# A network kernel on one core, with its list scheduler driven by the time-line model

## The chip, the cores and the metric

The kernel runs on one core of one Trainium2 chip. A core has TensorE (PE in the profile; its weight loads are PEld), VectorE (DVE), ScalarE (ACT), GpSimd (POOL) and SyncE (SP), which here issues DMAs. Each engine works through its own queue of instructions in order and waits on semaphores for the others. The metric is device time in microseconds of one execution; the kernel before takes 3337.39 us in the median of three runs (3337.23 to 3337.42).

## What is computed

The input x is 512 tokens by 1024 channels, float32. Four blocks follow one another; each has a mixer and a feed-forward part, joined by residual adds and RMS norms:

- layer 0: dilated attention (8 heads, three branches) beside latent attention with low-rank queries and keys; then a gated feed-forward network, modulated by six vectors that come from `silu(c) @ ada_w`;
- layer 1: a spatial gating unit beside a 2-D neighbourhood attention (8 heads); then a gated feed-forward network;
- block 2: an RWKV-7 time mix (16 heads of 64) beside a conformer convolution (31 taps along the tokens), with gates;
- block 3: mLSTM heads (4) and differential attention heads (4), a per-layer embedding, and a feed-forward network with a convolution.

The recurrence of block 2 is, per head, with k̂ the normalised key:

```
S_t = S_{t-1} diag(w_t) - (S_{t-1} k̂_t)(k̂_t * a_t)^T + v_t k_t^T
y_t = S_t r_t          # then a group norm per head, a bonus term and a gate
```

The kernel computes it in 8 chunks of 64 tokens. Within a chunk everything is matrix products, once a small triangular system has been inverted; from chunk to chunk the state S must be carried in order.

## The kernel before

Activations are held transposed, channels on partitions, as tiles of 128x512. Every weight matrix is streamed from HBM in slabs by SP's DMAs (L108). A slab is split in two reduced-precision parts, `whi` (a cast on ACT, L117) and `wlo` (a subtraction on DVE or POOL, L118), and each product takes three matmuls on PE (L123, L124, L125, with the activation split alike in `hhi` and `hlo`). "GEMM matmul" below means one of these three. They accumulate in PSUM tiles `psg`.

Block 2 handles the RWKV heads in pairs, p = 0 to 7. One pair has three parts:

- `rwkv_prep` makes the operands of its 8 chunks.
- `rwkv_invert` sends the triangular blocks through DRAM into another layout (`dram_L` to `uL`, L1147 and L1157), inverts them in some 20 small DVE steps (L1171, L1172), sends the result back through DRAM (`dram_DT<-uX`), and finishes on PE (`ps_D` L1211, `ps_T` L1217, `ps_X` L1225).
- `rwkv_steps` walks the chunks. One chunk is a chain over three engines: PE `ps_v` (L1248, L1250 with the state S), a copy of one half on DVE (L1251) and of the other on ACT (L1252) into `zV`, PE `ps_u` (L1255), ACT copy into `VU` (L1256), PE `ps_s` (L1259), DVE update of S (L1261). PE also adds to the output `ps_y` (L1253, L1264). After the eighth chunk comes the group norm: 8 squares on ACT (L1273), a row of small DVE operations (L250 to L256, L1276), 8 scalings on ACT (L1278), and four PE transposes `ps_yt` (L1281), read by DVE (L1283).

While these chains wait, other work is to fill the engines ("filler"): the conformer's input product and its 30 taps per channel tile on DVE (L1305, on tiles `z`), and the gates' products. The program lists them per pair in a string (`order`) and gives them a lower priority, by `high_priority(offset=self.fill_offset)` with an offset of -3000. The same device is used in layer 0, layer 1 and block 3, where attention heads run beside the next projection's or the gates' products. In block 3 a head's score block is: PE `ps_s` (L1635), DVE minimum (L1639), ACT exponential (L1641), a product on POOL (L1647), a sum on DVE (L1648), PE transposes `ps_pt` (L1651), an ACT copy (L1653), PE `ps_pv` (L1656); after four blocks come a head norm and transposes `ps_hdt` (L1619).

None of the queues' orders is written out by hand. The program records instructions in program order with their dependencies and priorities. A list scheduler then orders them: it steps a simulated machine through time, and whenever an engine is free there, it gives it the instruction of highest priority among those that are ready. A few manual edges (`issue_after`) tie fillers to a place. So the orders depend on what the simulated machine says is ready, and when.

## Time and profile before

| | |
|---|---|
| median of three runs | 3337.39 us |
| the profiled execution | 3332.78 us |
| its span (first to last instruction) | 3331.0 us |
| PE busy | 3179.2 us (95%) |
| DVE busy | 2041.3 us (61%) |
| ACT busy | 1386.5 us (42%) |
| POOL busy | 515.1 us (15%) |
| mean granted clock of PE | 0.983 of full speed |

A busy time is the union of an engine's instructions. Matmuls overlap one another in the pipeline, so their own durations sum to more than the busy time. The granted clock is 1.00 when PE runs at 2.4 GHz and 0.50 when it runs at 1.2 GHz; a stretch's figure is a mean of the two.

### The profile page before, as it was taken

How to read it: one execution, taken by the hardware profiler on the slowest of the kernel's cores; microseconds unless marked ns; L12 is line 12 of the kernel's file. 1: busy time of each engine (PE TensorE's matmuls, PEld its weight loads, DVE VectorE, ACT ScalarE, POOL GpSimd, SP SyncE). 2: the span in 40 equal slices, each digit the busy share in tenths (PEclk: the TensorE clock that was granted, in tenths of full speed). 3: DMA queues.
4: the chain of work that ended last, by engine and by line, in shares of the span. 5: the costliest groups of instructions: out<-in, count | busy, mean ns of one | idle time of the engine just before them, and what ended most of it. 6: DMA issues, size and time to landing. Idle time of an engine off the chain costs nothing. (4 is left out here: it accounts for less than half of the span.)

```text
span 3331.0 us, 43197 instructions
## 1 busy us (share of the span) xinstructions
PE 3179.2 (95%) x15337; PEld 2471.1 (74%) x15337; DVE 2041.3 (61%) x4002; ACT 1386.5 (42%) x2784; POOL 515.1 (15%) x603
## 2 busy tenths in 40 slices
PE   8999999999999999898899889999999999999998
PEld 6755778788778887666666656788877777788887
DVE  4576764654665356688778875434367764575665
ACT  3466332333443233454444444433244553343444
POOL 1000010111211011222223323111010011110111
PEclk9999999999999999999999999999999999999999
DMA  4411553525223332322122343233233125332322
GB/s 134 120 62 50 172 169 128 176 97 149 68 83 95 100 97 76 103 63 68 52 68 66 101 134 113 85 96 95 95 92 112 55 84 164 110 95 95 95 95 82
DMA packets 275032, 332.60 MB, mean 100 GB/s; under 512 B 52956, under 2 KB 188058, under 8 KB 274817
## 3 DMA queue, kind: packets, MB, share of 16 engines
q1 hardware_dynamic: 237392, 301.43, 29.4%
q10 hardware_dynamic: 33489, 12.39, 1.5%
q0 software_dynamic: 3936, 16.03, 1.5%
q8 instruction: 121, 1.98, 0.2%
q14 instruction: 94, 0.77, 0.1%
HBM read 311.88 MB, written 23.89 MB: 101 GB/s over the span
## 5 line engine op out<-in xcount | busy, mean ns | idle before, releaser
L118 DVE TENSOR_TENSOR wlo<-raw,whi 128x512 fp32r<-128x512 f32 (+2 forms) x865 | 625.2, 734 | 752.7 <-PE psg L124 419.3
L123 PE MATMUL psg<-hhi,whi 128*128 128x512 f32 (+1 forms) x2624 | 1044.5, 401 | 36.4 <-DVE glu L1301 7.0
L125 PE MATMUL psg<-hhi,wlo 128*128 128x512 f32 (+1 forms) x2624 | 1038.9, 397 | 13.3 <-DVE wlo L118 7.9
L124 PE MATMUL psg<-hlo,whi 128*128 128x512 f32 (+1 forms) x2624 | 1041.2, 397 | 0.0
L117 ACT CAST whi<-raw 128x512 fp32r<-128x512 f32 (+2 forms) x975 | 581.7, 604 | 1072.6 <-PE psg L124 924.6
L123 PEld LDWEIGHTS psg<-hhi,whi 128*128 128x128 f32 (+1 forms) x2624 | 496.5, 189 | 162.8 <-issue 17.2
L125 PEld LDWEIGHTS psg<-hhi,wlo 128*128 128x128 f32 (+1 forms) x2624 | 496.7, 189 | 124.9 <-POOL wlo L118 9.6
L124 PEld LDWEIGHTS psg<-hlo,whi 128*128 128x128 f32 (+1 forms) x2624 | 497.1, 189 | 107.2 <-issue 7.6
L123 PE MATMUL psg<-hidhi,whi 128*128 128x512 f32 x784 | 308.4, 394 | 1.0 <-DVE ffu L574 0.8
L125 PE MATMUL psg<-hidhi,wlo 128*128 128x512 f32 x784 | 308.0, 393 | 0.0
L124 PE MATMUL psg<-hidlo,whi 128*128 128x512 f32 x784 | 305.9, 390 | 0.0
L1305 DVE SCALAR_TENSOR_TENSOR z<-glu,par_B,z 128x512 f32<-128x512 f32 x240 | 197.0, 835 | 1.5
L118 POOL TENSOR_TENSOR wlo<-raw,whi 128x512 fp32r<-128x512 f32 (+1 forms) x110 | 146.8, 1341 | 281.3 <-ACT whi L117 217.3
L125 PEld LDWEIGHTS psg<-hidhi,wlo 128*128 128x128 f32 x784 | 147.2, 188 | 34.0
L124 PEld LDWEIGHTS psg<-hidlo,whi 128*128 128x128 f32 x784 | 147.2, 188 | 33.4
L123 PEld LDWEIGHTS psg<-hidhi,whi 128*128 128x128 f32 x784 | 147.4, 188 | 32.8 <-DVE ffu L574 1.3
L581 POOL TENSOR_TENSOR ffu<-ffu,ffg 128x512 f32<-128x512 f32 x44 | 64.7, 1469 | 582.6 <-DVE ffu L574 582.6
L1374 POOL TENSOR_TENSOR ffr<-ffr 128x512 f32<-128x512 f32 x32 | 40.1, 1261 | 293.0 <-ACT ffr L1373 286.9
L194 ACT CAST hidhi<-ffu 128x512 fp32r<-128x512 f32 x66 | 41.0, 622 | 106.1 <-POOL ffu L581 66.2
L195 DVE TENSOR_TENSOR hidlo<-ffu,hidhi 128x512 fp32r<-128x512 f32 x66 | 57.3, 868 | 30.9 <-ACT hidhi L194 29.4
L765 DVE SCALAR_TENSOR_TENSOR adacc<-adraw,c_act,adacc 128x1024 f32<-128x1024 f32 x42 | 53.9, 1284 | 33.4 <-DMA adraw<-in_ada_w_dram 33.0
L209 POOL TENSOR_TENSOR ss<-ss,sq 128x512 f32<-128x512 f32 x24 | 35.2, 1467 | 218.1 <-ACT sq L208 202.0
(572 smaller groups left out, 4040.3 us busy)
## 6 DMA issues: line engine op xcount, KB each, us to landing
raw<-in_ffn_w_gu_dram SPq DMA_DIRECT2D x176, 256.0 KB
raw<-in_w_in_dram SPq DMA_DIRECT2D x59, 512.0 KB
adraw<-in_ada_w_dram SPq DMA_DIRECT2D x48, 512.0 KB
raw<-in_w_up_dram SPq DMA_DIRECT2D x88, 256.0 KB
raw<-in_ffn_w_down_dram SPq DMA_DIRECT2D x42, 512.0 KB
raw<-in_w_ff_in_dram SPq DMA_DIRECT2D x32, 512.0 KB
raw<-in_w_ff_out_dram SPq DMA_DIRECT2D x32, 512.0 KB
raw<-in_w_in_dram SPq DMA_DIRECT2D x96, 128.0 KB
```

What stands on the lines that cost most here:

```text
L117: nc.scalar.copy(oi(hi), ri(r))
L118: eng.tensor_tensor(out=oi(lo), in0=ri(r), in1=fr(oi(hi)), op=ALU.subtract)
L123: first = nc.tensor.matmul(ps, lhsT=whi, rhs=xhi, start=start, stop=False)
L124: nc.tensor.matmul(ps, lhsT=whi, rhs=xlo, start=False, stop=False)
L125: nc.tensor.matmul(ps, lhsT=wlo, rhs=xhi, start=False, stop=stop)
L194: nc.scalar.copy(hi, t)
L195: nc.vector.tensor_tensor(out=lo, in0=t, in1=fr(hi), op=ALU.subtract)
L209: (nc.gpsimd if c < 4 else nc.vector).tensor_tensor(out=ss, in0=ss, in1=sq, op=ALU.add)
L581: nc.gpsimd.tensor_tensor(out=t, in0=t, in1=part[c], op=ALU.mult)
L765: nc.vector.scalar_tensor_tensor(out=acc, in0=raw, scalar=c[:, k:k + 1], in1=acc, op0=ALU.mult, op1=ALU.add)
L1305: tap = nc.vector.scalar_tensor_tensor(out=z[i], in0=g[:, j:j + T], scalar=cw(j), in1=z[i], op0=ALU.mult, op1=ALU.add)
L1374: nc.gpsimd.tensor_tensor(out=t, in0=t, in1=t, op=ALU.mult)
```

## The change

One argument is added where the program's context is made. The list scheduler then orders all queues with a time-line model of the engines, in place of its usual simulated machine.

```
-    with tile.TileContext(nc) as tc:
+    with tile.TileContext(nc, schedule_with_timeline_sim=True) as tc:
```

The two programs hold the same matmuls, vector operations and DMAs (PE 13741, DVE 4001, POOL 608, SP 943 instructions in both); what differs is the order in the queues, the waits that follow from it, and the number of ACT table loads (47, where it was 35). Three places show the kind of move.

On PE, in the fifth RWKV group (p = 4), from the `ps_u` of one chunk towards that of the next. Before:

```order
L1255 MATMUL ps_u_14484<-zV1_10969,zD0_10970 64x128
L123 MATMUL psg_15457<-hhi3_10779,whi_15498 128x512
L124 MATMUL psg_15457<-hlo3_10780,whi_15498 128x512
L125 MATMUL psg_15457<-hhi3_10779,wlo_15499 128x512
L1259 MATMUL ps_s_14487<-VU_14223,KB_14210 128x128
L1264 MATMUL ps_y_14458<-VU_14223,MLR_14180 64x64 x2
L123 MATMUL psg_15458<-hhi2_10773,whi_15494 128x512
L124 MATMUL psg_15458<-hlo2_10774,whi_15494 128x512
L125 MATMUL psg_15458<-hhi2_10773,wlo_15495 128x512
L123 MATMUL psg_15458<-hhi3_10779,whi_15498 128x512
L1248 MATMUL ps_v_14496<-VU_14223,MLR_14180 64x64 x2
L1250 MATMUL ps_v_14496<-S_14417,ar_14173 64x64 x2
```

And after, from the same `ps_u` (14484) on:

```order
L1255 MATMUL ps_u_14484<-zV1_10969,zD0_10970 64x128
L1259 MATMUL ps_s_14487<-VU_14223,KB_14210 128x128
L1264 MATMUL ps_y_14458<-VU_14223,MLR_14180 64x64 x2
L1248 MATMUL ps_v_14496<-VU_14223,MLR_14180 64x64 x2
L1250 MATMUL ps_v_14496<-S_14417,ar_14173 64x64 x2
L1253 MATMUL ps_y_14495<-S_14417,ar_14173 64x128
L1255 MATMUL ps_u_14504<-zV0_10968,zD0_10970 64x128
L1259 MATMUL ps_s_14507<-VU_14223,KB_14210 128x128
L1264 MATMUL ps_y_14495<-VU_14223,MLR_14180 64x64 x2
```

The GEMM matmuls on `psg` that stood in every gap of the chain are gone from this place. They now stand in blocks of about 20 in the gaps of the first chunks of the group. Counted over the eight groups, 34 of the 56 steps from one chunk to the next have no GEMM matmul in between (3, 3, 5, 3, 5, 4, 7 and 4 by group); before there was none of that kind.

On DVE, in the same group, from one `zV` copy to the next. Before, steps of the next pair's inversion stand there:

```order
L1251 COPY zV0_10968<-ps_v_14496 64x64
L1171 TENSOR_TENSOR uT_14891<-uX_14883,uM_14892 128x384
L1172 TENSOR_REDUCE uX_14883<-uT_14891 128x6x8
L1171 TENSOR_TENSOR uT_14891<-uX_14883,uL_14882 128x384
L1261 SCALAR_TENSOR_TENSOR S_14417<-S_14417,GC_13997,ps_s_14507 64x64 x2
L1172 TENSOR_REDUCE uX_14883<-uT_14891 128x2x8
L1251 COPY zV1_10969<-ps_v_14513 64x64
```

After, the same stretch holds seven convolution taps:

```order
L1251 COPY zV0_10968<-ps_v_14496 64x64
L1305 SCALAR_TENSOR_TENSOR z6_10986<-glu_15125,par_B_5986,z6_10986 128x512
L1305 SCALAR_TENSOR_TENSOR z7_10987<-glu_15128,par_B_5986,z7_10987 128x512
L1305 SCALAR_TENSOR_TENSOR z6_10986<-glu_15125,par_B_5986,z6_10986 128x512
L1305 SCALAR_TENSOR_TENSOR z7_10987<-glu_15128,par_B_5986,z7_10987 128x512
L1261 SCALAR_TENSOR_TENSOR S_14417<-S_14417,GC_13997,ps_s_14507 64x64 x2
L1305 SCALAR_TENSOR_TENSOR z6_10986<-glu_15125,par_B_5986,z6_10986 128x512
L1305 SCALAR_TENSOR_TENSOR z7_10987<-glu_15128,par_B_5986,z7_10987 128x512
L1305 SCALAR_TENSOR_TENSOR z6_10986<-glu_15125,par_B_5986,z6_10986 128x512
L1251 COPY zV1_10969<-ps_v_14513 64x64
```

The inversion of a pair now stands a whole group earlier (that of pair p+2 behind the group norm of pair p). Runs of three or four taps on each side of the state update stand in 13 of the 34 steps without GEMM matmuls (groups 0, 2 and 4); in the other 21, DVE has little beside the chain.

On PE, at the end of block 3's attention heads (`ps_s`, `ps_pt`, `ps_pv` and `ps_hdt` belong to the heads). Before:

```order
L1651 MATMUL ps_pt_23626<-ident_81,dP_23611 128x128 x3
L123 MATMUL psg_22468<-hhi6_20641,whi_22575 128x512
L124 MATMUL psg_22468<-hlo6_20642,whi_22575 128x512
L125 MATMUL psg_22468<-hhi6_20641,wlo_22576 128x512
L1656 MATMUL ps_pv_23632<-dv_20704,dPT_23630 128x128 x3
L123 MATMUL psg_22468<-hhi7_20645,whi_22579 128x512
L124 MATMUL psg_22468<-hlo7_20646,whi_22579 128x512
L125 MATMUL psg_22468<-hhi7_20645,wlo_22580 128x512
L1651 MATMUL ps_pt_23656<-ident_81,dP_23641 128x128 x4
L123 MATMUL psg_22469<-hhi6_20641,whi_22575 128x512
L124 MATMUL psg_22469<-hlo6_20642,whi_22575 128x512
L125 MATMUL psg_22469<-hhi6_20641,wlo_22576 128x512
```

After:

```order
L1656 MATMUL ps_pv_23603<-dv_20704,dPT_23601 128x128 x2
L1619 MATMUL ps_hdt_23400<-ident_81,hd_tm_23399 128x128 x4
L1651 MATMUL ps_pt_23626<-ident_81,dP_23611 128x128 x3
L1656 MATMUL ps_pv_23632<-dv_20704,dPT_23630 128x128 x3
L1651 MATMUL ps_pt_23656<-ident_81,dP_23641 128x128 x4
L1656 MATMUL ps_pv_23663<-dv_20704,dPT_23661 128x128 x4
L1619 MATMUL ps_hdt_23552<-ident_81,hd_tm_23551 128x128 x4
L123 MATMUL psg_23821<-hhi4_23717,whi_23827 128x512
L124 MATMUL psg_23821<-hlo4_23718,whi_23827 128x512
L125 MATMUL psg_23821<-hhi4_23717,wlo_23828 128x512
L123 MATMUL psg_23821<-hhi5_23721,whi_23831 128x512
L124 MATMUL psg_23821<-hlo5_23722,whi_23831 128x512
```

Before, the gates' GEMM matmuls stand between the last blocks, and some 260 more behind them. After, these have gone ahead of the heads' second half, the last ten blocks stand without them, and the next GEMM in the queue is one that reads the heads' results. In layer 1, in the same way, 24 of the 32 blocks of the neighbourhood attention (L711, L726, L738) stand without GEMM matmuls.

## Rows read from the trace of the kernel before

**Rows 1.** The page, part 1: busy time, share of the span, instructions.

```profile
PE 3179.2 (95%) x15337; PEld 2471.1 (74%) x15337; DVE 2041.3 (61%) x4002; ACT 1386.5 (42%) x2784; POOL 515.1 (15%) x603
```

**Rows 2.** Busy time by stage: stretch, length, engines, PEclk, DMA share, GB/s.

```profile
0.00:1312.00 1312.00, 1276.40 (x5837) 991.54 (x5837) 745.12 (x1333) 513.71 (x949) 140.41 (x148) 1.00 0.36 112
1312.00:1427.00 115.00, 96.39 (x497) 74.36 (x497) 81.01 (x169) 49.92 (x83) 33.45 (x60) 0.90 0.29 84
1427.00:2051.00 624.00, 554.28 (x3452) 398.80 (x3450) 495.40 (x1069) 302.71 (x798) 178.86 (x201) 0.95 0.29 82
2051.00:2112.00 61.00, 58.94 (x261) 47.27 (x261) 28.06 (x43) 20.07 (x36) 19.56 (x15) 1.00 0.32 99
...
2580.00:2760.00 180.00, 177.12 (x839) 132.85 (x838) 122.86 (x444) 91.35 (x253) 17.78 (x26) 1.00 0.24 70
```

**Rows 3.** What PE waited for: us in total, times, longest.

```profile
PE ps_u L1255 <- ACT zV L1252: 18.6, 7, 5.9
```

**Rows 4.** Time line of one chunk, last group: start, us, engine, line, operation.

```profile
2033.88 0.34 PE L1248 MATMUL ps_v<-VU,MLR 128*64 128x64 f32 x4
...
2034.04 0.29 PE L1250 MATMUL ps_v<-S,ar 128*64 128x64 f32 x4
...
2034.16 0.38 PE L1253 MATMUL ps_y<-S,ar 128*64 128x128 f32 x2
2034.38 0.22 DVE L1251 COPY zV<-ps_v 64x64 f32<-64x64 f32 x1 [1.07 <-PE ps_v L1250]
...
2034.68 0.21 ACT L1252 COPY zV<-ps_v 64x64 f32<-64x64 f32 x1 [0.56 <-DVE zV L1251]
2034.81 0.39 PE L124 MATMUL psg<-ya,whi 128*128 128x512 f32 x1
...
2035.04 0.40 PE L125 MATMUL psg<-ya,wlo 128*128 128x512 f32 x1
...
2035.37 0.43 PE L1255 MATMUL ps_u<-zV,zD 128*64 128x128 f32 x2
...
2035.84 0.26 ACT L1256 COPY VU<-ps_u 64x128 f32<-64x128 f32 x1 [0.31 <-PE ps_u L1255]
...
2036.54 0.38 PE L1259 MATMUL ps_s<-VU,KB 128*128 128x128 f32 x2
...
2036.85 0.45 PE L1264 MATMUL ps_y<-VU,MLR 128*64 128x64 f32 x4
2036.96 0.59 DVE L1261 SCALAR_TENSOR_TENSOR S<-S,GC,ps_s 64x64 f32<-64x64 f32 x2 [0.63 <-PE ps_s L1259]
```

**Rows 5.** The convolution taps, by line: least, median, longest ns.

```profile
L1305 DVE SCALAR_TENSOR_TENSOR z<-glu,par_B,z x240: 730/742/2415, 1411.2 to 1921.7; 128x512 f32<-128x512 f32 x120
```

**Rows 6.** Time line of the last group's group norm, its first and last PE row.

```profile
2039.62 0.43 PE L1255 MATMUL ps_u<-zV,zD 128*64 128x128 f32 x2
...
2051.04 0.33 PE L1281 MATMUL ps_yt<-ident,Y 128*128 128x128 f32 x1 [1.83 <-ACT Y L1278]
```

**Rows 7.** The chain that ended last: start, us, what.

```profile
1927.56 11.65 DMA uL<-dram_L
...
1973.61 9.69 DMA dram_DT<-uX
```

**Rows 8.** Block 3's heads by line, 2580 to 2760 us: busy, mean ns, idle before.

```profile
L1635 PE MATMUL ps_s<-dk,dq 128*128 128x128 f32 (+3 forms) x64 | 22.8, 452 | 1.2 <-DVE mn L1639 1.1
L1641 ACT ACTIVATE dP<-dP,mn 128x128 f32<-128x128 f32 (+3 forms) x32 | 17.9, 560 | 12.6 <-DVE mn L1639 9.9 <-DVE den L1644 1.2 <-DVE rs_o L256 0.9
L1639 DVE CUSTOM_DVE_ANT_0 dP<-ps_s,toepD 128x128 f32<-128x128 f32 (+3 forms) x32 | 15.2, 481 | 2.3 <-PE ps_pt L1651 1.5 <-PE ps_num L1593 0.6
...
L1647 POOL TENSOR_TENSOR dP<-dP,den 128x128 f32<-128x128 f32 (+3 forms) x16 | 12.2, 765 | 135.8 <-DVE den L1642 127.5 <-DVE rs_t L255 3.0 <-DVE rs_t L254 2.7
...
L1648 DVE SCALAR_TENSOR_TENSOR dP<-dP,den 128x128 f32<-128x128 f32 (+3 forms) x16 | 8.8, 550 | 1.0
```

**Rows 9.** Layer 1's neighbourhood attention by line, 850 to 940 us.

```profile
L711 PE MATMUL ps_s<-k,q 128*128 128x256 f32 x64 | 19.7, 401 | 0.0
L718 ACT ACTIVATE P<-P,mn 128x256 f32<-128x256 f32 x32 | 16.1, 504 | 8.5 <-DVE mn L716 8.2
```

## The prediction

> **What bounds the kernel now.** I read the busy shares first. TensorE is busy 95% of the span, DVE 61%, ACT 42% [rows 1]. So 3331.0 - 3179.2 = 152 us of PE idle time is all that a better order could win, as PE's work is the same in both programs.
>
> Next the same table by stage [rows 2], to see where these 152 us lie. In the first 1312 us PE idles 35.6 us; in block 3's heads (2580 to 2760) 2.9 us of 180. In block 2 it idles 115 - 96.39 = 18.6 us before the recurrence begins, 624 - 554.28 = 69.7 us during its eight groups, and 2.1 us behind them: 90.4 us in 800, well over half of all. There DVE is at 495 of 624 us, and the granted clock is 0.95, and 0.90 in the stretch before it, against 1.00 elsewhere.
>
> Then PE's waits: the longest single wait of the whole program is that of `ps_u` for the copy into `zV` [rows 3], a hop of the recurrence. So PE is the bound nearly everywhere; in block 2 it is PE together with a serial chain, and the GEMM matmuls in the chain's gaps keep PE busy. The time line of one chunk shows this [rows 4]: a GEMM matmul starts every 0.23 us (2034.81, 2035.04) between the `zV` copies and `ps_u`, and again between `ps_u` and `ps_s`.
>
> **The change, part by part.** No instruction on PE, DVE or POOL is added or removed. The sum is made in PE's idle time: what PE idles in the new order, less the old.
>
> *Chunks without GEMM matmuls, DVE free (21 steps).* Such a step lasts as long as the chain. From rows 4: `ps_u` to the start of the ACT copy 2035.84 - 2035.37 = 0.47; the copy 0.26; `ps_s` to the state update 0.42; the update 0.59; `ps_v` (L1250) to the DVE copy 0.34; that copy 0.22; 0.08 to the ACT copy; 0.21 for it. Together 2.59 us. Three hops into PE are missing, since GEMM matmuls stand there now. The shortest hop of these rows is 0.08, the longest 0.47 (it includes a matmul); I take 0.2, near the shorter, as nothing is queued ahead. The step is 3.2 us (2.8 to 4.0). PE works in it for 0.66 (L1248 to L1253) + 0.43 + 0.38 + 0.45 = 1.9 us. Idle: 1.3 us (0.9 to 2.1), times 21 = 27 us (19 to 44).
>
> *The same with taps on DVE (13 steps).* DVE has seven taps, one `zV` copy and the pair of updates: 7 x 0.742 [rows 5] + 0.22 + 0.59 [rows 4] = 6.0 us. In order on one engine this is a floor. If the taps lengthen the chain by all their time, it is 3.2 + 5.2 = 8.4. The taps stand on both sides of the update, where the chain is away from DVE, so I take the floor. Idle: 6.0 - 1.9 = 4.1 us, times 13 = 53 us (53 to 84).
>
> *Group norm (7 groups).* From the last `ps_u` to the first transpose the last group takes 2051.04 - 2039.62 = 11.4 us [rows 6], a chain on ACT and DVE. In the new order PE has there some 30 to 40 small matmuls of the next pair's preparation; a transpose of that size lasts 0.33 us [rows 6] and overlaps its neighbours, so I estimate 6 us, under 0.2 each. Before, GEMM matmuls filled this time. Idle 5.4 us, times 7 = 38 us; between 0, if the next group's first chunk fills it, and 80, if PE's small matmuls wait too.
>
> *Chunks with blocks of GEMM matmuls (22 steps).* The chain waits there for PE, not PE for the chain: no idle time in principle. But blocks of 20 matmuls, 4.5 us, meet a DVE whose taps and weight splits (L118) were ordered for a model, and PE waits for the difference. By the present stage's 69.7 us over its 56 steps, 1.2 us a step, this is between 0 and 27 us; I take 15.
>
> *Before and behind the recurrence.* More filler stands ahead of the first `ps_u` than now: idle 12 us in place of 18.6 (0 to 18.6); behind it 2 as now.
>
> *The inversion a group earlier.* The two DMA waits on today's chain, 11.65 and 9.69 us [rows 7], go from the way between two groups. What is late next is the group norm counted above. PE had filler during these waits, so I give no gain beyond that the 69.7 us are taken off whole.
>
> Sum for block 2: 27 + 53 + 38 + 15 + 12 + 2 = 147 us, less 90 = +57.
>
> *Clock.* Today the granted clock falls to 0.90 and 0.95 in just the stretches where PE idles 16% and 11% of the time, and is 1.00 where it idles less than 4% [rows 2]: part of each runs at 1.2 GHz. With 147 us idle in some 860 (17%) I take 0.92 for the recurrence in place of 0.95. That is 3% of 554 us, 17 us of PE time, of which half lies where PE is the bound: +8 (0 to 20). The Trainium skill speaks of this too ("TensorE: Matmul & The Clock Gate", Part 1: the clock is set by how busy PE was of late, so idle time is paid for twice); the trace agrees, 0.90 at 16% idle. By its rule alone every long bare run falls to the lower level, and its PE time, 34 x 1.9 = 65 us, would double, at most +65 in place of +8.
>
> *Block 3's heads.* Ten score blocks stand bare. One block needs on DVE 2 x 0.481 + 0.550, some 2 us with its small operations; on ACT 2 x 0.560 and a copy; its chain (0.452 PE, 0.481 DVE, 0.560 ACT, 0.765 POOL, 0.550 DVE, then two PE steps and a copy) is some 5 us [rows 8], and PE works in it for 2.3. If blocks overlap until DVE is full, PE loses about 0.3 us a block, 3 us in all; one after another, 47 with hops. The queue keeps two blocks apart, so I take 1.2 a block, and 4 for the last head norm, behind which the next GEMM has to wait: +16.
>
> *Layer 1.* 24 of 32 blocks bare. ACT holds 2 operations of 0.50 in most [rows 9], about 1.1 us a block with the copies; PE 0.8 to 1.4. Between 0 and 16 us; I take 8. *Layer 0's heads* lose filler alike, by layer 1's numbers 0 to 10, taken 5. The GEMM stages keep their order but for a few rows: 0, cover being the weight loads far ahead (DMA share 0.36 [rows 2]).
>
> Total: 57 + 8 + 16 + 8 + 5 = +94. On the profiled execution, 3332.8, this gives 3427; the median of the runs lies 4.6 us above that execution, so 3432.
>
> The Trainium skill ("Perfetto Trace Analysis", Optimization Strategy) says that where the most-contended engine changes over time, interleaving those regimes may help. The new order does the reverse within each group: GEMM blocks first, then chain alone. The same page (Identifying the Most-Contended Engine) holds that PE's busy share is no measure of its room, weight loading is; here that is 74% [rows 1]. By that, a better order could win more than my 152 us; no row here shows it.
>
> **The rivals.**
>
> *Not slower: the shorter groups win.* The mechanism: today's 69.7 us arise mostly at group changes, where inversion, DMA round trips [rows 7] and group norm follow one another; with the inversion a group ahead, the next group's first GEMM-filled chunks begin right behind the norm, and DVE does its taps where PE works anyway. For it: 21 us of DMA in one group change. Against: PE is busy in 554 of the 624 us, so these changes are well filled today. It decides at the 13 steps with taps: if these cost nothing over the chain (1.3 us idle as the others, 17 in place of 53) and the filled steps and the start are without idle time, block 2 has 27 + 17 + 38 + 2 = 84, under the 90 of today, and with norms half covered 65: -25, no clock loss, the heads at 3 to 10. The time is about 3320.
>
> *A small loss.* Group changes and bare chunks cancel, and only the heads count: 16 + 8 + 5 = +29, 3366. For it: the bounds of the norm reach 0.
>
> *A larger loss.* In the filled steps the engines' queues no longer fit: a tap or split that waits for a PE block holds up the state update behind it on DVE, and PE then waits as long. At 4.5 us, one block, in 16 of the 22 steps this is +72 over the forecast: 3504. With the upper bounds of tapped steps (+31) and clock (+12) it is near 3550. For it: DVE has 495 us of work in the 624 [rows 2], little slack if it comes in lumps.
>
> *No change.* The chip's own waits level the orders out. Against: 34 steps without filler against none.
>
> **How the numbers follow.** Forecast (3385 to 3475): 0.50. Larger loss (above 3475): 0.19. Small loss (3344 to 3385): 0.15. Within 0.2%, 6.7 us, about what a measurement of this kernel tells from no change: 0.04. Faster: 0.12. So slower is 0.50 + 0.19 + 0.15 = 0.84. The range from 3340 to 3545 leaves out the faster case, half of no change and a quarter of the larger loss, about 0.19.
>
> **What would show it.** In the trace after: PE idle in block 2 near 147 us, with steps of about 3.2 us where chunks are bare and 6.0 where taps stand; the longest PE waits at `ps_u`, `ps_s` and `ps_yt`, the releaser of tapped steps being DVE; a group norm of about 11 us; a granted clock under 0.95 in the recurrence; no DMA waits between groups; block 3's heads with some 15 us more PE idle time. The forecast is wrong if block 2's PE idle time stays under 90 us, or if PE's time outside the stages named grows by more than 15 us.

## The result

The kernel after takes 3566.86 us in the median of four runs, the kernel before 3337.31 us beside it: a ratio of 1.0691, 95% interval 1.0672 to 1.0709. It is slower by some 230 us. The direction was forecast, the size was not: 3432 us, with 3545 as the upper end. The profiled execution has a span of 3562.1 us, 231 more than before, and its busy shares already show that something is missing from the forecast's method:

```profile
PE 3251.3 (91%) x15337; PEld 2556.1 (72%) x15337; DVE 2073.6 (58%) x4002; ACT 1399.4 (39%) x2796; POOL 517.2 (15%) x603
```

With the same matmuls, PE is busy 72 us more than in [rows 1]. By stage, against [rows 2] (stretch, length, busy time of PE, PEld, DVE, ACT and POOL, granted clock, DMA share, GB/s):

```profile
0.00:1349.00 1349.00, 1288.71 (x5832) 1003.89 (x5832) 754.12 (x1332) 513.08 (x949) 138.60 (x145) 0.99 0.36 109
1349.00:1494.00 145.00, 127.26 (x640) 102.78 (x641) 101.14 (x195) 62.44 (x102) 48.81 (x73) 0.89 0.29 85
1494.00:2276.00 782.00, 589.54 (x3343) 436.36 (x3341) 488.33 (x1048) 294.67 (x783) 178.19 (x195) 0.80 0.22 65
2276.00:2340.00 64.00, 56.46 (x241) 45.14 (x241) 27.11 (x56) 18.42 (x33) 15.28 (x12) 0.90 0.24 75
```

Up to block 2 the kernel is 37 us late (1349 for 1312). In block 2, the last three rows, it takes 991 us for 800 and so loses 191 more, 158 of them in the recurrence, 782 us for 624. There the granted clock is 0.80 where it was 0.95. Behind block 2 the two differ by a few us. (The 30 us by which the stretch ahead of the recurrence grew are PE at work, 127 us for 96, mostly on matmuls that stood further back before.)

The eight groups of the recurrence can be cut at the first `ps_u`, at the first step without GEMM matmuls, at the last `ps_u` and at the first `ps_yt`. Summed over the groups (lengths and busy times from the stage tables of these stretches, GEMM matmuls counted in the time line):

| | before: us, PE idle, GEMM matmuls | after |
|---|---|---|
| steps with filler | 335, 30, 530 | 348, 34, 1027 |
| bare steps | none | 178, 75, 1 |
| group norms | 178, 28, 504 | 117, 42, 36 |
| group changes (`ps_yt` to next `ps_u`) | 111, 11, 233 | 139, 41, 124 |

So 1027 of 1188 GEMM matmuls now stand in 348 us, and the other 434 us hold 161 of them: 37 us of such work at 0.23 us each. (Counted so, from `ps_u` to `ps_u`, there are 33 bare steps after and 2 before, not 34 and none.)

One group, p = 4, in this cut (same columns as above: filled steps, bare steps, norm, change):

```profile
1934.20:1971.70 37.50, 32.34 (x159) 24.63 (x158) 34.01 (x60) 14.55 (x30) 11.11 (x15) 0.95 0.31 84
1971.70:1999.10 27.40, 15.09 (x92) 9.64 (x92) 26.80 (x52) 3.38 (x18) 0.21 (x1) 0.60 0.03 11
1999.10:2014.80 15.70, 9.98 (x58) 8.55 (x57) 11.63 (x28) 8.27 (x29) 9.30 (x6) 0.61 0.05 8
2014.80:2041.10 26.30, 18.61 (x129) 13.18 (x129) 12.87 (x35) 14.22 (x30) 1.11 (x4) 0.81 0.23 71
```

In the bare steps DVE is the one that is full (26.80 of 27.40); in the norm and the change nobody is.

A bare step with DVE free, in group 3, against [rows 4] (start, us, engine, line, operation, idle time before and what ended it):

```profile
1891.63 0.43 PE L1255 MATMUL ps_u<-zV,zD 128*64 128x128 f32 x2 [0.38 <-ACT zV L1252]
1892.10 0.26 ACT L1256 COPY VU<-ps_u 64x128 f32<-64x128 f32 x1 [0.52 <-PE ps_u L1255]
1892.41 0.49 PE L1259 MATMUL ps_s<-VU,KB 128*128 128x128 f32 x2 [0.35 <-ACT VU L1256]
...
1892.94 0.59 DVE L1261 SCALAR_TENSOR_TENSOR S<-S,GC,ps_s 64x64 f32<-64x64 f32 x2 [1.66 <-PE ps_s L1259]
...
1893.67 0.34 PE L1248 MATMUL ps_v<-VU,MLR 128*64 128x64 f32 x4 [0.40 <-DVE S L1261]
1893.81 0.32 PE L1250 MATMUL ps_v<-S,ar 128*64 128x64 f32 x4
...
1894.16 0.22 DVE L1251 COPY zV<-ps_v 64x64 f32<-64x64 f32 x1 [0.64 <-PE ps_v L1250]
1894.47 0.21 ACT L1252 COPY zV<-ps_v 64x64 f32<-64x64 f32 x1 [0.64 <-DVE zV L1251]
1894.73 0.32 PE L1255 MATMUL ps_u<-zV,zD 128*64 128x128 f32 x1 [0.41 <-ACT zV L1252]
```

From `ps_u` to `ps_u` this takes 1894.73 - 1891.63 = 3.10 us: the forecast's 3.2. Later steps of the same kind, at the lower clock, take 3.9. In group 4 the same chain has the taps between its two DVE operations:

```profile
1979.03 0.57 DVE L1261 SCALAR_TENSOR_TENSOR S<-S,GC,ps_s 64x64 f32<-64x64 f32 x2 [0.21 <-PE ps_s L1259]
1979.63 2.08 DVE L1305 SCALAR_TENSOR_TENSOR z<-glu,par_B,z 128x512 f32<-128x512 f32 x3
...
1981.74 0.22 DVE L1251 COPY zV<-ps_v 64x64 f32<-64x64 f32 x1
1981.88 2.06 DVE L1305 SCALAR_TENSOR_TENSOR z<-glu,par_B,z 128x512 f32<-128x512 f32 x3
...
1982.31 0.69 PE L1255 MATMUL ps_u<-zV,zD 128*64 128x128 f32 x2 [1.40 <-ACT zV L1252]
```

DVE has no gap, and the step takes some 5.5 us (6.0 forecast: taps in a run take 0.69 us each, not 0.74). And the change of group 4, on PE alone, shows what the forecast had not priced:

```profile
2019.26 1.06 PE L1211 MATMUL ps_D<-ident,zD 128*128 128x128 f32 x4
2020.12 1.77 PE L1056 MATMUL ps_w<-WD,tw 128*128 128x128 f32 x8
2028.25 2.08 PE L1061 MATMUL ps_a<-alo,WA 128*128 128x512 f32 x2 [6.36 <-DVE bon L1143]
2030.26 1.73 PE L1217 MATMUL ps_T<-D,zC 128*32 128x32 f32 x32
...
2033.12 1.10 PE L1225 MATMUL ps_X<-zD,zT 128*32 128x32 f32 x32
...
2041.10 0.32 PE L1255 MATMUL ps_u<-zV,zD 128*64 128x128 f32 x1
```

`ps_T` and `ps_X`, which the next group's first step needs, stand behind `ps_a` of a later pair's preparation, and `ps_a` waits for DVE. DVE itself waits there for a DMA. In its queue the first copy of a later pair's inversion, `uM`, stands ahead of `bon`, the operation that releases `ps_a`, and the data of that copy are still on their way through DRAM:

```profile
2025.55 0.15 POOL L1161 MEMSET uL<- 128x32 f32 x1 [15.78 <-DMA uL<-dram_L]
2025.74 0.29 DVE L1177 COPY uM<-uL 128x256 f32<-128x256 f32 x1 [7.79 <-POOL uL L1161]
...
2027.51 0.68 DVE L1143 TENSOR_TENSOR bon<-ps_bon,xs_v 128x512 f32<-128x512 f32 x1
```

In front of this copy DVE stands idle in five of the seven group changes, 5.3 to 7.8 us each, 34 us in all; in three of them (groups 1, 3 and 4) `bon` and `ps_a` stand behind it. In the kernel before, these waits, but for the first pair's, lay inside the steps of a group, where PE had GEMM matmuls. In group 6 the same copy stands ahead of the update of S, and behind that the conformer's norm (L1343) ahead of the `zV` copy; this step takes 16.9 us:

```profile
2132.18 1.34 DVE L1177 COPY uM<-uL 128x256 f32<-128x256 f32 x1 [5.22 <-POOL uL L1161]
...
2134.74 0.57 DVE L1261 SCALAR_TENSOR_TENSOR S<-S,GC,ps_s 64x64 f32<-64x64 f32 x2
2135.34 4.17 DVE L1343 TENSOR_TENSOR z<-z,RSTD 128x512 f32<-128x512 f32 x5
...
2143.65 0.21 DVE L1251 COPY zV<-ps_v 64x64 f32<-64x64 f32 x1
```

A second step of group 6 takes 15.5 us: ACT's copy into `zV` stands behind work that waits for the inversion's other DMA, on its way back:

```profile
2171.93 2.92 ACT L1351 ACTIVATE z<-z,par_B 128x512 f32<-128x512 f32 x4 [3.60 <-DMA zD<-dram_DT]
2174.88 0.21 ACT L1252 COPY zV<-ps_v 64x64 f32<-64x64 f32 x1
2175.14 0.69 PE L1255 MATMUL ps_u<-zV,zD 128*64 128x128 f32 x2 [10.38 <-ACT zV L1252]
```

PE's waits in block 2, 1349 to 2340 us, against the one of [rows 3] (us in total, times, longest):

```profile
PE ps_u L1255 <- ACT zV L1252: 46.8, 37, 10.4
PE ps_M L1117 <- ACT zK L1113: 23.5, 6, 4.3
PE ps_a L1061 <- DVE bon L1143: 23.3, 5, 6.4
PE ps_v L1248 <- DVE S L1261: 20.9, 33, 6.6
PE ps_s L1259 <- ACT VU L1256: 15.4, 33, 2.3
PE ps_yt L1281 <- ACT Y L1278: 14.3, 20, 7.8
```

The first, fourth and fifth are the chain (83 us). The second and third are a later pair's preparation (47 us): all six waits of `ps_M` lie in the group norms, and 18 of the 23 us of `ps_a` in the group changes. The last is the norm.

### The profile page after: what moved, and what is told of

Read it like the earlier page. It is cut to its first block, busy times and chain, and to the rows that moved or that the text cites. A ratio compares the mean times of both kernels' runs of the same rounds, so it can differ in the third digit from the quotient of the medians.

```text
span 3562.1 us, 43196 instructions
## 1 busy us (share of the span) xinstructions
PE 3251.3 (91%) x15337; PEld 2556.1 (72%) x15337; DVE 2073.6 (58%) x4002; ACT 1399.4 (39%) x2796; POOL 517.2 (15%) x603
## 5 line engine op out<-in xcount | busy, mean ns | idle before, releaser
L125 PE MATMUL psg<-hhi,wlo 128*128 128x512 f32 (+1 forms) x2624 | 1002.5, 396 | 8.2 <-DVE wlo L118 5.6
L1305 DVE SCALAR_TENSOR_TENSOR z<-glu,par_B,z 128x512 f32<-128x512 f32 x240 | 186.9, 813 | 1.9
L1255 PE MATMUL ps_u<-zV,zD 128*64 128x128 f32 x128 | 36.4, 378 | 46.8 <-ACT zV L1252 46.8
```

The lines of the kernel that those rows point to most:

```text
L125: nc.tensor.matmul(ps, lhsT=wlo, rhs=xhi, start=False, stop=stop)
L1255: nc.tensor.matmul(psu[64:128, 0:128], lhsT=XT[:, c, :], rhs=Vb, start=True, stop=True)
L1305: tap = nc.vector.scalar_tensor_tensor(out=z[i], in0=g[:, j:j + T], scalar=cw(j), in1=z[i], op0=ALU.mult, op1=ALU.add)
```

## The experiments

Most of them need a queue's order to be laid down. A table of instruction numbers is added to the kernel, and each instruction of it is tied behind the one before it by an edge that sets the issue order and adds no wait (the code is shortened here):

```
+def queue_as(tc, table):
+    for steps in table:                       # one list per queue
+        for ins, prev in zip(steps[1:], steps):
+            tc.add_manual_dep(ins, prev.name, DependencyInfo(NoSync, DATA), reason="issue order")
...
             Net(tc, ctx, a).run(out)
+            queue_as(tc, ORDER)
```

The differences below are between medians: of a run to the kernel after (3566.9), or to the kernel before as measured beside the run (3334 to 3338).

### Which stage: block 2 put back, and block 2 alone

`ORDER` holds all five queues of block 2, as in the kernel before, in the kernel after; and the reverse.

> The kernel after, but every queue's instructions of block 2 are tied (issue order only) into the order that the kernel before has; all other stages stay as the time-line model orders them. Theory A (the loss sits in block 2's order: of the 229 us, 187 lie between the last feed-forward product of layer 1 and the end of block 2, the rest, 44, in layer 0, its modulation and block 3): 3380 us, 3370 to 3395, with the granted clock in the recurrence back at 0.95 and its PE idle time back near 70 us. Rival B (block 2 loses because of what reaches it, weights late or another state of the clock after a slower start, whatever its own order): over 3450.

> The opposite: the kernel before, but block 2's queues in the order of the kernel after. Theory A: 3337 + 187 = 3524 us, 3510 to 3540, with a granted clock of 0.80 in the recurrence. Rival B: under 3450.

Measured: 3375.6 us (191 less than the kernel after, ratio to before 1.0110, 1.0095 to 1.0125) and 3518.0 us (181 more than before, ratio 1.0539, 1.0523 to 1.0555). Theory A holds on both sides, rival B falls. Four fifths of the loss go with block 2's order, whatever reaches it.

### Which queue of block 2

`ORDER` holds PE's queue alone, DVE's alone, or both, as in the kernel before, in the kernel after; then DVE's alone, as in the kernel after, in the kernel before.

> The kernel after, but of block 2 only PE's queue is tied into the order of the kernel before; DVE, ACT, POOL and SP are ordered by the time-line model round it. Theory A in its narrow form (what counts is that PE has GEMM matmuls between the hops): within 25 us of e1, 3370 to 3405. Rival C (the taps and inversions on DVE, as the model puts them, hold the chain wherever PE's matmuls stand): 3450 or more.

> The kernel after, but of block 2 only DVE's queue is tied into the order of the kernel before; PE, ACT, POOL and SP are ordered by the time-line model round it, and PE's queue still has 35 steps without GEMM matmuls. Theory G (half the loss of block 2 is DVE's: it has 101, 65, 92, 30, 85, 34 and 48 us of work in the first seven groups of the kernel after, where the kernel before has 56 to 78 in each; the groups with taps wait for DVE, the others for the chain): the gain that PE's order alone did not bring, about 100 us, 3450 to 3490. Rival H (what counts is PE's bare steps): they are still there, 3530 to 3570.

> The kernel after with block 2's PE and DVE queues as in the kernel before, ACT, POOL and SP free. Theory G: PE's and DVE's order explain block 2 together, within 15 us of the run with all queues as before: 3365 to 3391. Rival I (ACT's or SP's order, with the inversion's DMAs issued from ACT and the group norm on ACT, holds a part): 3405 or more.

> The opposite of the first: the kernel before, with only block 2's DVE queue in the order of the kernel after. PE's queue, ordered by the usual machine round it, then has 25 steps without GEMM matmuls by itself. Theory G: 100 to 180 us slower than before, 3437 to 3517, with DVE's work as uneven over the groups as in the kernel after. Rival H (DVE's order is harmless unless PE's is bunched by the time-line model): under 3400.

Measured: 3475.2 us for PE (92 less than the kernel after), 3501.1 for DVE (66 less), 3380.9 for both (186 less), and 3571.0 for DVE's order in the kernel before (233 more, ratio 1.0700, 1.0684 to 1.0717). The narrow form of theory A falls, since PE's order alone brings half, and rival C's figure came (3450 or more). With DVE's order put back the time lies between the ranges of theory G (up to 3490) and rival H (from 3530), so neither holds there; in the reverse run rival H falls, and theory G's 3517 is passed by 54 us. Rival I falls, as ACT, POOL and SP hold some 5 us. The two orders together explain block 2, and they don't add up: 92 + 66 = 158, not 186. The last run shows this too: DVE's order alone costs more than all queues together did (181), and the usual machine then bunches PE's queue too. So the grouping of the work is in DVE's order as much as in PE's.

With PE's order put back, the group norm is what stretches. PE's waits in its block 2:

```profile
PE ps_yt L1281 <- ACT Y L1278: 45.0, 5, 16.9
PE ps_u L1255 <- ACT zV L1252: 30.4, 13, 6.9
PE ps_v L1248 <- DVE S L1261: 20.1, 9, 6.3
```

### Is it the clock?

Matmuls that compute nothing are added to the bare steps. In the first run they stand behind `ps_v`, `ps_u` and `ps_s` and write unused columns of the same tiles; in the second there are fewer, in columns of `ps_y` that nothing reads.

```
+            SPUN.append((self.nc.tensor.matmul(ps[:, 128:256], lhsT=self.ident, rhs=self.ident, start=True, stop=True).ins, after.ins.name))
...
+            SPUN.append((self.nc.tensor.matmul(ps[yo, 256:384], lhsT=self.ident[:, 0:64], rhs=self.ident, start=False, stop=False).ins, after.ins.name))
```

> The kernel after with block 2's order tied as it is, plus 631 matmuls of 128 columns that compute nothing, behind ps_v, ps_u and ps_s of the steps without GEMM matmuls (12 in a step, 24 in those with taps, 18 in group 6), where PE waited. Their results go to unused columns; the chain and the order are unchanged. Theory D (part of the loss is the clock: PE falls to 1.2 GHz in the bare steps, and norms and group changes behind them run at that level, 62 us more PE busy time): faster than the kernel after by 25 to 60 us, 3507 to 3542, granted clock of the recurrence above 0.88. Rival E (the low clock only goes along with idle time and costs nothing on the chain): no change within 10 us, or slower by what the added matmuls take, 0.11 us each or 69 us in all where they don't fit, 3557 to 3635.

> The run before this (spin_in_bare_steps) held the clock at 1.00 in the bare steps but put the added matmuls on the chain, since the readers of ps_v, ps_u and ps_s waited for them. Here there are fewer (6 in an ordinary bare step, 12 in a tapped one, 9 in group 6; each is two of 0.11 us) and they write unused columns of ps_y, which the chain doesn't read. Order and chain as in the kernel after. Theory D (the low clock costs time of its own, as chain hops, norms and group changes run at 1.2 GHz): 20 to 60 us faster than the kernel after, 3507 to 3547. Rival E (the chain is held by DVE, ACT and hops, so the low clock lengthens PE's records and little else): 3555 to 3580, though the clock of the bare steps rises above 0.85.

Measured: 3664.9 us and 3563.8 us. The first lies above both ranges and tells nothing of the clock's worth: each added matmul counted as two on the chip, and DVE and ACT waited for them, as they read the same tiles; the bare steps grew from 178 to 269 us. The second is the answer. Its recurrence:

```profile
1494.00:2278.00 784.00, 619.64 (x3953) 481.57 (x3952) 488.58 (x1055) 296.16 (x788) 175.70 (x193) 0.88 0.22 64
```

The granted clock rises from 0.80 to 0.88, in the bare steps from 0.58 to 0.92, and the time falls by 3 us, within the spread of the runs. Step by step, the six bare ones of groups 1, 5 and 7 that took 3.9 us take 3.11 to 3.23, those with taps stay at 5.49, and all bare steps together go from 178 to 172 us, the norms from 117 to 112; the filled steps and changes take back as much. Theory D falls, rival E stands, for what this run lifts: in norms and changes the clock stays below 0.9, and the added matmuls take PE time of their own. The kernel after has steps of the same work at either level, first two bare ones with DVE free, then two with taps:

```profile
1891.63:1894.73 3.10, 1.94 (x19) 1.23 (x19) 0.78 (x3) 0.99 (x6) 0.00 (x0) 1.00 0.00 0
2093.55:2097.46 3.91, 3.24 (x19) 2.06 (x19) 0.78 (x3) 0.99 (x6) 0.00 (x0) 0.50 0.00 0
1971.72:1977.18 5.46, 1.97 (x20) 1.25 (x19) 5.38 (x11) 0.47 (x2) 0.00 (x0) 1.00 0.15 54
1982.31:1987.80 5.49, 3.22 (x18) 2.04 (x18) 5.41 (x11) 0.47 (x2) 0.00 (x0) 0.50 0.00 0
```

At the lower clock PE is busy 1.3 us longer; a free step grows by 0.8 us, a step that DVE fills by next to nothing.

### What holds the chain: dealing PE's filler out, cutting the taps

In the kernel after, PE's filler of each group is dealt evenly over the 21 gaps of its chunks (`ORDER` holds PE's queue alone). Then the taps are cut to 8 columns, with all queues tied as they are, in the kernel after and in the kernel before:

```
-                tap = nc.vector.scalar_tensor_tensor(out=z[i], in0=g[:, j:j + T], scalar=cw(j), in1=z[i],
+                tap = nc.vector.scalar_tensor_tensor(out=z[i][:, 0:8], in0=g[:, j:j + 8], scalar=cw(j), in1=z[i][:, 0:8],
```

> The kernel after, but PE's queue in block 2 has the same instructions of each group dealt evenly over the 21 gaps of its 8 chunks (between ps_u, ps_s and ps_v) instead of in the first chunks; nothing moves from one group to another or out of the norm; DVE, ACT, POOL and SP are free. Theory A (bunching within a group is the cause): steps with and without filler, 526 us with 110 idle in the kernel after, shrink by 80 to 110 us: 3455 to 3490. Rival C (DVE's and ACT's order, with taps and norms, holds the chain): it stays above 3520.

> The kernel after with block 2's queues tied as they are, but every convolution tap works on 8 of its 512 columns, so the convolution's output is left out but for those. No instruction moves. Theory J (the taps, which stand in groups 0, 2 and 4 alone, hold the chain there, and the group norms behind them): the tapped steps fall from 5.5 to about 3.5 us and the first four groups of steps by more, together 60 us or more: 3505 or less. Rival K (it is the inversion and the preparation, put a group ahead, that load DVE and delay norm and next group; the taps fill time that is lost anyway): 3535 or more.

> The same cut in the kernel before, queues tied as they are. By theory J the taps lie beside PE's work there: 0 to 20 us faster than before, 3317 to 3337. By rival K as well. If it gains as much as the run before this, the taps cost the same in both orders and are no cause of the difference.

Measured: 3532.6 us dealt evenly (34 less than the kernel after); 3531.5 with cut taps (35 less); 3307.6 with cut taps in the kernel before (31 less than before). Dealt evenly, theory A's 80 to 110 us did not come, and rival C's figure did (above 3520). With cut taps the kernel after lies between theory J (3505 or less) and rival K (3535 or more); theory J falls by the run beside it: the taps cost as much in the old order as in the new, so they explain nothing of the difference by themselves. The tapped steps did fall, by 24 us in all.

The stretches tell why dealing out brought so little: the steps went from 525 to 457 us, by 68 of theory A's 80 to 110, but the norms grew from 117 to 163. Group 4, dealt evenly, steps and norm:

```profile
1915.13:1967.86 52.73, 45.97 (x248) 31.66 (x249) 46.20 (x91) 18.25 (x48) 12.26 (x16) 0.90 0.24 66
1967.86:2000.07 32.21, 10.05 (x60) 8.55 (x59) 26.94 (x55) 9.69 (x31) 9.52 (x7) 0.65 0.07 21
```

DVE is busy 26.94 of the norm's 32.21 us; in the rest it waits for the inversion's DMA again (5.17 us in front of `uM`, ahead of the norm's last operations). The kernel before has 38, 46, 37, 41, 35 and 33 of the 240 taps in its first six groups; the kernel after has 67, 30, 60, 0, 60 and 0 (so not groups 0, 2 and 4 alone, as the expectations say, but most of them there). Dealt evenly, 22, 28 and 23 taps run inside the norms of groups 0, 2 and 4, which take 31, 37 and 32 us; groups 1, 3 and 5 have none there and take 11 to 13. The steps are over sooner, the taps are not, and they stand on DVE ahead of the norm's operations. So both cuts at once, and filler for the norm without touching DVE:

> Both cuts at once: PE's queue of block 2 dealt evenly within each group (alone: 34 us) and the taps on 8 of 512 columns, so that the convolution's output is left out but for those (alone: 35 us in the kernel after, 31 in the kernel before). Theory G (two limits, one behind the other: in groups 0, 2 and 4 DVE has more than PE once PE is dealt evenly, so either cut alone only brings the other limit forward): clearly more than the sum, 100 us or more, 3467 or less. Rival K (neither is the limit; inversion and preparation a group ahead hold norms and group changes): about the sum, 3490 to 3510.

> The kernel after with PE's queue of block 2 dealt evenly over the gaps of the chunks and a third of each group's filler put behind its last chunk, where the group norm left PE idle for 98 us in the evenly dealt run. Taps whole. If the idle norm is PE's lack of filler alone: 40 to 70 us faster than that run, 3460 to 3495. Theory G (DVE, late with its taps in groups 0, 2 and 4, makes the norm late there, and PE's filler then lies beside it but does not shorten it): 10 to 35 us faster, 3498 to 3523, with the norms of groups 0, 2 and 4 still over 25 us.

Measured: 3478.2 us for both cuts, 89 less than the kernel after, and 3508.8 with filler behind the last chunk, 24 less than dealt evenly. The second is as theory G has it; the norms of groups 0, 2 and 4 stay at 39, 34 and 38 us. The first lies between the two: more than the sum (69), less than theory G's 100. With both cuts the norm of group 4 is nearly as short as those without taps:

```profile
1882.30:1927.81 45.51, 43.46 (x248) 30.02 (x248) 32.34 (x116) 18.97 (x49) 14.35 (x19) 0.96 0.28 76
1927.81:1941.26 13.45, 8.00 (x59) 6.47 (x58) 5.79 (x20) 8.89 (x30) 3.85 (x4) 0.87 0.06 11
```

So the two limits do stand one behind the other, and they are not all. Against the kernel before with cut taps (3307.6) this kernel still loses 171 us, and 133 without the 38 of the other stages. Its norms and changes, 253 us, hold 162 us of PE's busy time, where the kernel before with cut taps has 242 in 270; the work that left them stands in the steps, 441 us for 328. In its first six changes DVE waits 48 us in front of `uM`, up to 10.8 at once; in five of them PE's `ps_D` waits for an operation behind that copy, 24 us in all. What of these 133 us is the inversion's wait and the preparation in the changes, and what the filler drawn out of norms and changes, was not told apart, as no run moved either alone; the orders of the kernel before bring back both.

### The other stages, each alone in the kernel before

`ORDER` holds one stage's queues as in the kernel after.

> The kernel before, with layer 0's queues alone in the order of the kernel after. Theory A (the losses of the stages add up, each by its own order): the first product of the feed-forward network starts 18 to 20 us later in the kernel after, so 3337 + 19 = 3356, 3350 to 3362. Rival F (part of it is given back later, as the feed-forward network loads its weights earlier in that time): under 3348.

> The kernel before, with only the first feed-forward network and the modulation in it ordered as in the kernel after: the modulation's 48 DMAs of 512 KB and its DVE sums stand in the first quarter of the weight stream in place of the first half. Theory A: the rest of the 38 us at its end, 3337 + 19 = 3356, 3348 to 3364, with PE waits of ps_ada on DVE's sums, 16 us in the kernel after. Rival F (the modulation only waits because layer 0 ended late): within 7 us of 3337.

> The kernel before, with only block 3's mixer in the order of the kernel after (bare score blocks at the end of its heads). Theory A: the kernel after loses 6 us between there and its end, so 3343, within 3339 to 3349. My forecast's term of 16 us would be 3353.

Measured: layer 0 3359.2 us (+25, ratio 1.0072, 1.0059 to 1.0085), the first feed-forward network 3357.3 (+23, ratio 1.0070, 1.0055 to 1.0085), block 3's mixer 3352.5 (+15, ratio 1.0047, 1.0035 to 1.0060). Theory A holds for the first two. For block 3 it falls, and the forecast's own 16 us is right for that stage alone. Alone they make 62 us; with block 2 as before they and layer 1 make 38 together. So they don't add up: a stage that follows a late one finds more of its weights loaded; this is the likely reason, and it was not tested. In the run of the feed-forward network PE's longest wait there is one that the kernel before doesn't have in its list:

```profile
PE ps_ada L770 <- DVE adacc L765: 14.6, 4, 4.6
```

The transposes of the modulation stand early in PE's queue, each in front of the network's matmuls, while DVE still waits for the weights to sum (34 us for their DMAs). What takes layer 0's 25 us was not told apart.

## Why the prediction was wrong

The slowdown was forecast, its size was not. Two steps failed: "the inversion a group earlier", which took the DMA waits off the way between two groups, and the sum in idle time. Step by step:

- **"The inversion a group earlier. The two DMA waits [...] go from the way between two groups. [...] What is late next is the group norm counted above": this step failed.** The group change behind the norm was given nothing. It grew from 111 to 139 us, though 109 GEMM matmuls left it, and PE idles 41 us in it instead of 11. The DMA waits went into it: in five of seven changes DVE stands idle for `uL<-dram_L` (34 us), and in three of them `bon`, `ps_a` of a later pair's preparation, and the next pair's `ps_T` and `ps_X` stand behind that. It was to be read in the order: DVE's queue has `uM` ahead of `bon` there, PE's has `ps_w` and `ps_a` between `ps_D` and `ps_T`. This is read from the trace. The runs show that PE's and DVE's orders make up the loss of block 2; what this wait is worth in it no run shows.
- **The bare steps: right in groups 0 to 5 and 7, wrong in group 6.** 3.2 and 6.0 us a step were forecast; 3.1 to 3.9 (one 4.5) and some 5.5 came. But all 34 were to take 145 us and the trace has 178, and group 6 alone has the difference: 57 us for its seven steps, forecast at 22, one of 16.9 and one of 15.5. In the first DVE waits for the DMA of the inversion ahead of the update of S; in the second ACT waits for the inversion's other DMA ahead of its `zV` copy. That the idle time came out near the forecast, 75 us for 80, is luck: group 6 has 32 of it instead of 9, the others 43 instead of 71.
- **The clock: right in what it is worth.** +8 us; the run that lifted it from 0.80 to 0.88 gained 3. Its fall was deeper than the 0.92 assumed.
- **The group norm: too short by a quarter.** 11.4 us were forecast, 14.6 came (117 for eight), 42 us idle against 38 for seven. 24 us of this idle time are `ps_M` of a later pair's preparation, which waits for ACT.
- **"The sum is made in PE's idle time": this step hid the size.** Idle time in block 2 rose from 90 to 218 us (147 forecast), that is by 127; the time rose by 191. The rest, 64 us, is in PE's busy time, 773 us for 710, for the same matmuls. In the bare steps PE is busy 103 us where the forecast has 34 x 1.9 = 65, because it runs there mostly at the lower clock: a slower PE fills idle time in stretches that it doesn't bound, and makes them little longer (0.8 us a free step, next to nothing a step that DVE fills). Where the clock moves, idle time is no measure of what a stretch loses. The measure is the length of each stretch by its chain, against the GEMM matmuls in it: 434 us with 37 us of GEMM work, where the kernel before has 1267 such matmuls spread over 624.
- **The steps with filler: right in kind.** 15 us idle were forecast and 34 came; 348 us for 1027 GEMM matmuls and the preparation is PE at work.
- **Layer 0 and the modulation:** 5 and 0 forecast, 25 and 23 alone, 37 together (with layer 1) where block 2 begins. "Cover being the weight loads far ahead" looked at the wrong transfer for the modulation: not the weights of the GEMMs were late but its sums, with PE's transposes now queued too early for them.
- **Block 3 and layer 1:** 16 and 8 forecast; 15 alone for block 3, a few in the whole kernel. Layer 1 is 5 us later at the end of its attention and has given this back at the end of its feed-forward network.

One reading was off, and nothing in the sum rests on it: PE's waits at `ps_u` are the largest in total, but the longest single wait of the kernel before is one of 7.4 us, of a GEMM matmul for DVE's `wlo`.

The larger-loss rival came nearest, 3504 to near 3550 for 3567, with a mechanism near the true one: DVE's queue in lumps. Its place was wrong. It expected PE to wait in the filled steps; the loss sits in the bare steps, the norms and the changes.

The Trainium skill ("TensorE: Matmul & The Clock Gate", Part 1) says that the clock is set by how busy PE was of late. The trace agrees, 0.58 in the bare steps against 0.95 in the filled ones. What the clock costs is for the run to say: 3 us for the part that it lifted, where the forecast gave the rule up to 65. The rule of the Trainium skill ("Perfetto Trace Analysis", Optimization Strategy), that interleaving regimes may help, is borne out from its other side: block 2's new order, which pulls the GEMM matmuls and the chain apart, costs 5.4% by itself.

## What to carry to other kernels

Where a serial chain runs beside work that is bound by one engine, count that work in each stretch of the chain, before and after: a stretch that lost its filler costs its whole length, and neither the idle time nor the busy share of the engine says so when its clock moves. Read in the order what stands ahead of the next link of the chain at the change from one chain to the next, not only inside it, on every engine of the chain: an operation that waits for a DMA holds all that stands behind it in its queue. A wait that is moved earlier is not gone; look for what it now lies in front of. Put the queues back one at a time and together before a cause is named: here single cuts brought 34, 35, 66 and 92 us, and PE's and DVE's orders together 186.

## What the runs showed of the hardware

A matmul of float32 operands written once in the kernel ran as two on the chip, 0.11 us apart at 128 columns with the granted clock at 1.00: 630 added matmuls left 1260 records. Operations that read a tile waited for matmuls to other columns of it (ACT 81 us in all for those in `ps_u`); whether the chip or the waits that the program sets make it so was not told apart. A bare step with DVE free took 3.9 us at 1.2 GHz and 3.1 at 2.4; as the lower clock is half the higher, I estimate from the difference that its chain has some 0.8 us of clocked PE time. The inversion's data took some 10 us through `uL<-dram_L`, from 2015.44 to 2025.51 us in the change of group 4.
